# A 16384 x 2048 x 2048 product: B22 also by quarters, the next A11 B11 inside the A22 T4 block, PSUM as eight one-bank tiles, new slots for C

## The chip, the cores and the metric

One core of one Trainium2 chip. The metric is the device time of one execution in microseconds (us), the median of several runs. All runs told here were classed fast (but for the single one of `before_again`, whose state is unknown), so they are compared as they stand; a "slow" or "typical" run below is only the longer one of several fast ones. "The first kernel" below is the kernel before the change, "the changed kernel" the one after it.

In the lines of the profile PE is TensorE (PEld its weight loads), DVE VectorE, ACT ScalarE, POOL GpSimd and SP the engine that issues the transfers (DMAs). PSUM is the memory that TensorE writes its sums to; a bank of it holds one 128x512 tile in fp32. An eviction is the read of such a tile out of PSUM.

## The reference

```python
def setup_inputs():
    B, S, D = 8, 2048, 2048
    return {"x": np.random.randn(B, S, D).astype(np.float32),
            "w": np.random.randn(D, D).astype(np.float32)}

def reference(x, w):
    cs = np.cumsum(x, axis=1)
    diff = cs - np.concatenate([np.zeros(...), cs[:, :-1, :]], axis=1)
    return np.matmul(diff, w).astype(np.float32)
```

The difference of the running sum is x itself, so the kernel computes x (16384 x 2048) times w (2048 x 2048).

## The kernel before

The rows come in tiles of 128. Two row tiles make a pair, and a pair of row tiles with the halves of w is multiplied in Winograd's form of Strassen's scheme: seven products of half size in place of eight. In the code A11, A12 are the halves of the first row tile, A21, A22 those of the second; B11 to B22 are the quarters of w; S1 to S4 and T1 to T4 are sums of A and of B. One `product` is 16 matmuls of 128x512. Two pairs make a group (pair g and pair h); there are 31 groups. The first is "plain": it runs while the operands of the inner level are still being made.

In the other 30 groups some products are split once more ("by quarters"): pair g's A and pair h's A are taken as the two row blocks of an inner scheme. Seven inner products of 4 matmuls, 28 in all, take the place of two products of 16, 32 in all. The first kernel does this for A12 B21 of both pairs (`inner_2`) and for A22 T4 of both pairs (at the end). Every sum of products passes through an add in fp32 on VectorE, from PSUM into the output tile C.

```python
    cpool = ctx.enter_context(tc.tile_pool(name="C", bufs=4))
    psum4 = ctx.enter_context(tc.tile_pool(name="ps4", bufs=1, space=bass.MemoryType.PSUM))

    def product(ps, a, b, first):
        for k in range(KH):                                  # 8
            for n in range(NH // NB):                        # 2
                nc.tensor.matmul(ps[:, ds(n * NB, NB)], a[k], b[k][:, n, :],
                                 start=(first and k == 0), stop=(k == KH - 1), ...)

    def product_in(ps, a, b, first):
        for k in range(4):
            nc.tensor.matmul(ps, a[k], b[k], start=(first and k == 0), stop=(k == 3), ...)

    def keep(dst, ps, scale):                                # eviction on ScalarE
        after("act", lambda: nc.scalar.activation(dst, ps, COPY, scale=scale))

    def add(dst, ps, scale):                                 # eviction on VectorE
        after("dve", lambda: nc.vector.scalar_tensor_tensor(dst, ps, scale, dst, MUL, ADD))

    # less_in: the sums of an inner scheme's operands, 16 subtractions on VectorE
    # weigh: |x| summed over a row (ScalarE); ready: narrow to 16 bits, transpose by DMA

    def group(t0, X, Y, Z, V):                # X, Y, Z, V: PSUM tiles 128x1024, two banks
        g, h = t0, t0 + 2
        q, e = V[:, :NB], V[:, NB:]
        early = g == PLAIN
        # ... weigh(h + 1), ready(h + 1), units, sums_in(A12g, A12h)

        def inner_2():
            y, z = Z[:, :NB], Z[:, NB:]
            product_in(q, a11, t11, True)
            add(Cg[:, :NB], q, ug)
            product_in(y, a12, t21, True)
            add(Cg[:, :NB], y, ug)
            product_in(e, s1, Q1, True)
            product_in(q, s2, Q2, False)
            add(Cg[:, NB:], q, ug)
            # ... weigh(g + 4), ready(g + 4); s4 t22 and a22 Q4 with their adds
            product_in(q, s3, Q3, False)
            add(halves(Ch), both(q), uh)
            put(Ch, h, 0)

        product(X, A11g, B11, True); Cg = new_c(); keep(Cg, X, ug)
        # ... (the plain group: product(V, A12g, B21, True), less(T3, ...), sums(g), add)
        product(Y, A11h, B11, True); Ch = new_c(); keep(Ch, Y, uh)
        # ... (the others: sums(g), inner_2())

        def rest(t, X, S):
            S1, S2, S3, S4 = S
            product(X, S2, T2, False); C12 = new_c(); keep(C12, X, u0)
            product(Z, S1, T1, True);  C22 = new_c(); keep(C22, Z, u1)
            # ... weigh, ready
            product(X, S3, T3, False); add(C22, X, u1)
            put(C22, t + 1, 1)
            product(Z, S4, B22, False)                     # 16 matmuls for each pair
            add(C12, Z, u0)
            put(C12, t, 1)

        # ... sums(h), units; in the plain group also less(T4, ...) and less_in(in2)
        rest(g, X, Sg)
        # ... in the second group less_in(in4); sums_in(A22g, A22h)
        rest(h, Y, Sh)

        # A22 T4 of both pairs, by quarters
        product_in(q, a11, t11, True);          keep(Cg[:, :NB], q, vg)
        product_in(X[:, :NB], a12, t21, False)
        product_in(e, s1, Q1, True)
        product_in(q, s2, Q2, False);           keep(Cg[:, NB:], q, vg)
        # ...
        product_in(q, s3, Q3, False);           keep(halves(Ch), both(q), vh)
        add(Ch[:, NB:], e, vh); add(Ch, Y, vh); put(Ch, h + 1, 0)
```

## Time and profile before

| | first kernel |
|---|---|
| median of 3 runs | 1556.03 us (1555.99 to 1556.76) |
| TensorE busy | 1522.0 us, 98% of the span, 7020 matmuls |
| VectorE, ScalarE busy | 55%, 53% |
| one steady group | 46.69 us, 216 matmuls |
| waits of TensorE after the first 160 us | under 1 us in all |

Read it from the top: one engine is busy nearly all the time, its waits are nearly all at the start, and its pitch (0.2158 us a matmul) does not vary. The time is then the number of matmuls times the pitch, plus the start and the end. The lines behind this stand in the prediction.

### The profile page before, as it was taken

Reading aid. Unit: us, or ns where it says so; the run is one execution under the profiler, and the core shown is the slowest. Engines: PE = TensorE matmul, PEld = TensorE weight load, DVE = VectorE, ACT = ScalarE, POOL = GpSimd, SP = SyncE. Lnnn points to the kernel's source line nnn. Section 1 sums busy time; section 2 is a strip of 40 time slices with the busy share of each in tenths; the row PEclk is TensorE's granted clock in tenths of the full one; section 3 lists DMA queues with packets and bytes.
Section 4 is the critical chain, followed back from the end, with each engine's and each line's share of the span. In section 5 each row is a group of like instructions: output and inputs, shape, how many; then the busy total and the mean of one; then the engine's idle time right before and its main releaser. Section 6 shows DMA issues by size and latency. Waiting matters only on the chain.

```text
span 1555.1 us, 18082 instructions
## 1 busy us (share of the span) xinstructions
PE 1522.0 (98%) x7020; PEld 689.8 (44%) x7024; DVE 854.0 (55%) x1477; ACT 823.2 (53%) x712; POOL 7.3 (0%) x16
## 2 busy tenths in 40 slices
PE   6979999999999999999999999999999999999998
PEld 3434444444444444444444444444444444444443
DVE  5866656555456555456555456554456554456553
ACT  5774455555455555455555455555455555455541
POOL 0100000000000000000000000000000000000000
PEclk9999999999999999999999999999999999999999
DMA  9868777877777867777877777777777877777852
GB/s 360 316 176 247 219 224 226 247 209 232 214 226 222 249 210 231 215 226 220 247 213 232 215 228 218 247 213 232 216 227 216 247 214 232 216 228 215 247 171 98
DMA packets 319221, 351.41 MB, mean 226 GB/s; under 512 B 264736, under 2 KB 264736, under 8 KB 303136
## 3 DMA queue, kind: packets, MB, share of 16 engines
q1 hardware_dynamic: 317968, 346.07, 73.2%
q0 software_dynamic: 1168, 4.19, 0.7%
q8 instruction: 55, 0.90, 0.2%
q14 instruction: 30, 0.25, 0.0%
HBM read 150.99 MB, written 134.22 MB: 183 GB/s over the span
## 4 chain that ended last, share of the span: by engine, by line
PE 90%; DVE 0%; ACT 0%; issue 0%
PE Y L336 22%; PE X L336 22%; PE Z L336 22%; PE V L347 13%; PE X L347 3%; PE Z L347 3%; PE Y L347 3%; DVE c L375 0%; DVE W L384 0%; ACT c L371 0%; DVE xT L384 0%; DVE u L426 0%; DVE m L111 0%; DVE s L112 0%; ACT xT L105 0%
## 5 line engine op out<-in xcount | busy, mean ns | idle before, releaser
L336 PEld LDWEIGHTS <-W 128*128 128x128 f16 x2976 | 291.2, 98 | 351.2
L116 ACT ACTIVATE fin<-fin,s 128x2048 f16<-128x2048 f32 x124 | 248.2, 2002 | 130.8 <-issue 98.4
L336 PEld LDWEIGHTS <-xT 128*128 128x128 f16 x2048 | 200.8, 98 | 249.1 <-issue 9.1
L375 DVE SCALAR_TENSOR_TENSOR c<-V,u,c 128x512 f32<-128x512 f32 (+1 forms) x211 | 174.7, 828 | 185.9 <-ACT c L371 115.2
L105 ACT ACTIVATE xT<-fin 128x2048 f16<-128x2048 f32 x124 | 235.9, 1903 | 21.6 <-PE X L347 6.1
L336 PE MATMUL Z<-W,W 128*128 128x512 f16 x896 | 217.2, 379 | 0.0
L336 PE MATMUL X<-W,W 128*128 128x512 f16 x854 | 207.5, 379 | 0.0
L336 PE MATMUL Y<-W,W 128*128 128x512 f16 x854 | 207.5, 379 | 0.0
L371 ACT ACTIVATE c<-V,u 128x512 f32<-128x512 f32 (+1 forms) x90 | 74.6, 829 | 189.6 <-PE V L347 189.6
L336 PE MATMUL Y<-W,xT 128*128 128x512 f16 x688 | 157.2, 382 | 2.7 <-DMA xT<-fin 2.7
L336 PE MATMUL X<-W,xT 128*128 128x512 f16 x688 | 155.7, 379 | 2.4 <-DVE m L111 1.8
L375 DVE SCALAR_TENSOR_TENSOR c<-Y,u,c 128x1024 f32<-128x1024 f32 (+1 forms) x91 | 100.6, 1106 | 86.7 <-PE Y L336 47.9
L336 PE MATMUL Z<-W,xT 128*128 128x512 f16 x656 | 148.3, 379 | 0.0
L375 DVE SCALAR_TENSOR_TENSOR c<-Z,u,c 128x1024 f32<-128x1024 f32 (+1 forms) x93 | 103.2, 1110 | 81.5 <-PE Z L336 42.6
L347 PEld LDWEIGHTS <-W 128*128 128x128 f16 x960 | 93.7, 98 | 116.1 <-issue 6.4
L375 DVE SCALAR_TENSOR_TENSOR c<-X,u,c 128x1024 f32<-128x1024 f32 (+1 forms) x91 | 100.7, 1106 | 79.1 <-PE X L336 40.2
L111 DVE TENSOR_SCALAR m<-m 128x1 f32<-128x1 f32 x124 | 18.2, 147 | 227.7 <-ACT xT L105 227.7
L371 ACT ACTIVATE c<-Y,u 128x1024 f32<-128x1024 f32 x63 | 69.9, 1110 | 125.2 <-PE Y L336 125.2
L371 ACT ACTIVATE c<-X,u 128x1024 f32<-128x1024 f32 x63 | 70.0, 1110 | 120.5 <-PE X L336 118.9
L371 ACT ACTIVATE c<-Z,u 128x1024 f32<-128x1024 f32 x62 | 68.8, 1110 | 111.1 <-PE Z L336 111.1
L347 PE MATMUL V<-in,W 128*128 128x512 f16 x480 | 113.3, 379 | 0.3 <-DVE c L375 0.3
L347 PEld LDWEIGHTS <-xT 128*128 128x128 f16 x720 | 70.4, 98 | 85.0
(67 smaller groups left out, 1048.1 us busy)
## 6 DMA issues: line engine op xcount, KB each, us to landing
fin<-in_x_dram SPq DMA_DIRECT2D x125, 1024.0 KB, 6.6
out_dram<-c SPq DMA_DIRECT2D x248, 512.0 KB, 4.3
W<-in_w_dram SPq DMA_DIRECT2D x32, 512.0 KB, 9.7
out_dram<-o POOLq DMA_DIRECT2D x7, 512.0 KB, 3.8
W<-in_x_dram SPq DMA_DIRECT2D x12, 256.0 KB, 7.8
xT<-fin SPq DMA_TRANSPOSE x124, 4.3
out_dram<-o POOLq DMA_DIRECT2D x2, 256.0 KB, 4.1
```

The source lines that it names most:

```text
L105: return m, xT, nc.scalar.activation(xT.rearrange("p k m -> p (k m)"), xf, ABS, accum_out=m)
L111: nc.vector.tensor_scalar(m, m, TINY, 1.0 / ROW, MAX, MUL)
L116: return xh, nc.scalar.activation(xh, xf, COPY, scale=s)
L336: nc.tensor.matmul(ps[:, ds(n * NB, NB)], a[k], b[k][:, n, :], start=(first and k == 0), stop=(k == KH - 1), skip_group_check=True,)
L347: nc.tensor.matmul(ps, a[k], b[k], start=(first and k == 0), stop=(k == 3), skip_group_check=True)
L371: after("act", lambda: nc.scalar.activation(dst, ps, COPY, scale=scale))
L375: "dve", lambda: nc.vector.scalar_tensor_tensor(dst, ps, scale, dst, MUL, ADD)
```

## The change

Its intent: S4 B22 of the two pairs is also taken by quarters in 30 of the 31 groups, which saves 4 of 216 matmuls. This gives VectorE and ScalarE more to do, so the order is redone around it: PSUM becomes eight tiles of one bank each, so that a write to one bank never has to wait for a read of its neighbour; the A22 T4 block has its inner products in another order, with the next group's A11 B11 put between two of them; x tiles are weighed into a slot of C, and one of four into PSUM; C's slots are assigned by name.

```diff
+    def bank(i):
+        return psum.tile([P, NB], f32, name=f"b{i}")
@@ weigh: the waste goes into a slot of C, or (weigh_in) into two banks of PSUM
+            m, _ = after("act", lambda: measure(xf, new_c(slot)))
@@ product, keep, add: a list of two one-bank tiles in place of a two-bank tile
-                    ps[:, ds(n * NB, NB)],
+                    ps[n],
...
@@ rest: only the plain group keeps it; the others
+        product(X, S2, T2, False)
+        C12g = new_c(c)
+        keep(C12g, X, ug)
...
+        product(Z, S1, T1, True)
+        C22 = new_c(d)
+        keep(C22, Z, vg)
+        add(C12g, Z, ug)
...
+        inner_product(A2, in2, banks, C11g, C11h, *u, between_2)
...
+        if second:
+            less_in(*in3)
+        one, two, A3 = sums_in(S4g, S4h, S0, S3g)
...
+        inner_product(A3, in3, banks, C12g, C12h, *u, between_3)
+        put(C12h, h, 1)
...
+        if second:
+            less_in(*in4)
+        product(Y, S3h, T3, False)
...
@@ A22 T4, at the group's end
+        product_in(q, s2, Q2, False)
+        add(C21g[:, NB:], q, vg)
+        put(C21g, g + 1, 0)
+        weigh(h + 5, d)
+        if g + 4 < END:
+            product(X, parts(g + 4)[0], B11, True)
+        add(C21h[:, NB:], e, vh)
+        product_in(q, s3, Q3, False)
```

## The prediction

> **What bounds the kernel now.** I read the page's busy line first, then who made TensorE wait over the whole run, then three stretches of 140 us from the middle, then the order of single instructions.
>
> ```profile
> PE 1522.0 (98%) x7020; PEld 689.8 (44%) x7024; DVE 854.0 (55%) x1477; ACT 823.2 (53%) x712; POOL 7.3 (0%) x16
> ...
> PE 90%; DVE 0%; ACT 0%; issue 0%
> ```
>
> TensorE is busy 98% of the span and carries 90% of the chain that ended last. A busy PE need not be a PE at its best, so I checked two more things. First, what it waited for in all (us in total, times, longest):
>
> ```profile
> PE V L151 <- POOL eye masks.py:199: 10.6, 1, 10.6
> PE X L266 <- ACT W L245: 4.5, 5, 2.8
> PE Y L336 <- DMA xT<-fin: 2.7, 1, 2.7
> PE V L266 <- ACT W L245: 2.4, 3, 1.5
> PE X L336 <- DVE m L111: 1.8, 1, 1.8
> ...
> PE V L347 <- DVE c L375: 0.3, 1, 0.3
> ```
>
> All of these lie in the first 160 us (start-up, and the first group, which does without the inner level). Second, the pitch: in the chain a product of 16 matmuls takes 3.45 us, so one 128x512 matmul takes 0.2158 us, and that is the same in all three stretches, at full clock:
>
> ```profile
> 184.40:324.48 140.08, 140.08 (x649) 63.38 (x648) 75.13 (x132) 74.21 (x63) 0.00 (x0) 1.00 0.75 225
> 604.63:744.70 140.07, 140.07 (x650) 63.42 (x648) 75.12 (x132) 74.22 (x63) 0.00 (x0) 1.00 0.75 225
> ```
>
> The columns are PE, PEld, DVE, ACT, POOL busy, clock, DMA share and GB/s. Such a stretch holds three groups of two row pairs, 648 = 3 x 216 weight loads; with as many matmuls a group takes 140.08 / 3 = 46.69 us. The code says the same: two pairs of seven products of 16 are 224, less 4 where A12 B21 of both pairs is taken by quarters (7 x 4 = 28 for 2 x 16 = 32), less 4 for A22 T4. 216 x 0.2158 = 46.61, so only 0.08 us of a group is not matmuls at full pitch. Where it goes can be seen at a group's last inner products:
>
> ```profile
> 702.37 0.69 ACT L371 ACTIVATE c<-V,u 128x512 f32<-128x512 f32 x1 [2.30 <-PE V L347]
> 702.82 0.10 PEld L347 LDWEIGHTS <-W 128*128 128x128 f16 x1
> 703.11 1.89 PE L347 MATMUL V<-in,W 128*128 128x512 f16 x8
> ```
>
> The next product starts 703.11, just after the ACT read of V's first bank ends (703.06), though it writes V's second bank; at pitch it would have started at 702.17 + 4 x 0.2158 = 703.03. So the kernel is bound by the number of its matmuls, and DVE (75.13 / 3 = 25.0 us of 46.7 a group) and ACT (24.7 us) have room.
>
> **What the Trainium skill says.** "TensorE: Matmul & The Clock Gate", section "Back-to-back issue gap", gives N / 2.4 + 2.5 ns warm, 216 ns for N = 512; the trace agrees (215.8). (The section also gives about 131 ns for a sustained stream of 512-wide matmuls, which this trace doesn't show.) "PSUM — Partial Sum Buffer", section "PSUM bank collisions raise a hardware error", says two engines may not be in one bank and quadrant at once, reads against reads included. That concerns the change: keep(C22, Z) on ACT and add(C12, Z) on DVE now read the same Z banks after one product, so they must take turns; the trace of before has no such pair. "ScalarE: Activation LUTs", section "What ACT_TABLE_LOAD costs", gives an ACTIVATE a fixed part (186 ns, and 93 for each pointer operand) beside 0.833 ns an element, and 93 ns of overlap back to back. The trace agrees nearly: 687 ns for 512 and 1110 for 1024. An eviction in two halves is then dearer, 2 x 687 less 93 = 1281 against 1110.
>
> **The change part by part.**
>
> 1. Matmuls. In 30 of the 31 groups S4 B22 of both pairs goes from 2 x 16 to 7 x 4 = 28 matmuls: 4 fewer a group, 120 in all, at 0.2158 us = 25.9 us. All of that lies on the path that sets the end. A group should take 212 x 0.2158 = 45.75 us.
> 2. One-bank tiles. The wait of 0.08 us a group goes, since the bank written is no longer in the tile being read: 30 x 0.08 = 2.4 us. Moving A22 T4 to the group's end, with the next A11 B11 between (s2 Q2) and (s3 Q3), puts 3.45 us of other work between them and hides the read of their shared bank q.
> 3. DVE gets dearer. From the costs by shape:
>
> ```profile
> L375 DVE SCALAR_TENSOR_TENSOR c<-V,u,c 128x512 f32<-128x512 f32 x180 | 134.9, 750 | 150.6 <-ACT c L371 115.2 <-PE V L347 34.3
> L375 DVE SCALAR_TENSOR_TENSOR c<-Z,u,c 128x1024 f32<-128x1024 f32 x63 | 80.9, 1284 | 76.6 <-PE Z L336 42.6 <-ACT xT L105 31.9
> L384 DVE TENSOR_TENSOR W<-xT 128x512 f16<-128x512 f16 x61 | 25.4, 416 | 0.0
> ```
>
> A group gets a third inner block (7 adds of 0.75 and one of 1.28: 6.5 us), four adds of 1.284 each in two of 0.75 (+0.9), four more sums of 0.42 (+1.7), the last folds (+0.2) and one reduce (+0.2): 25.0 + 9.5 = 34.5 us, 75% of 45.75. Beside PE, if it comes in time.
> 4. ACT: 16 evictions of 0.69 = 11.0 us for the former 9.2, and one of the four ABS passes in four pieces into PSUM (about 3.2 for 2.1): 24.7 + 3 = 27.7 us, 61%. Not on the path.
> 5. One-time costs, estimated by following the program's order with these durations. Plain group: the sums of the second pair now stand behind the first pair's last add on DVE and have one set of S1, S2 slots, so PE waits about 0.2 + 1.4 + 0.2 + 1.4 = 3.2 us for S2; the 1.8, 0.6 and 0.3 us waits of before in that group go. The 2.7 us wait for the first transposes stays. About +0.5. Second group: the weighing and narrowing of a row tile stand ahead of the eviction of the first X (+1.5), and 32 operand subtractions instead of 16 come here (+1). Together +3.
> 6. The end. The last matmul of before (slot end 1547.9) is followed by three dependent steps:
>
> ```profile
> 1548.10 1.11 ACT L371 ACTIVATE c<-V,u 128x1024 f32<-128x1024 f32 x1 [1.90 <-PE V L347]
> 1549.24 0.75 DVE L375 SCALAR_TENSOR_TENSOR c<-V,u,c 128x512 f32<-128x512 f32 x1 [0.88 <-ACT c L371]
> 1550.03 1.28 DVE L375 SCALAR_TENSOR_TENSOR c<-Y,u,c 128x1024 f32<-128x1024 f32 x1
> ```
>
> After, one add of 1.28 us follows it: 1.9 us less; but in the last group nothing stands between (s2 Q2) and (s3 Q3), so PE waits about 1 us for the add between. Net -1.
>
> Sum: -25.9 - 2.4 + 3 - 1 = -26.3 us, 1529.7 us, were the steady groups free of new waits.
>
> **The rivals.**
>
> *DVE becomes the bound in the inner blocks.* In one, DVE has 7 adds and a wide one: back to back an add starts 0.66 us after the one before (721.01 and 721.67 in the timeline), so 7 x 0.66 + 1.28 = 5.9 us, for 28 matmuls of PE = 6.04 us. There is no room to catch up inside a block, and DVE enters the second and third blocks late, from add(C12, Z) that takes turns with ACT on Z and (second) three sums of 0.69 and add(C22, X). Following the order by hand, add q ends 0.3 to 0.45 us after PE wants bank q for (s2 Q2) in both blocks if reads take turns, 0.3 us before if they don't. At the worst 0.8 us a group, 30 x 0.8 = 24 us: the gain is gone, about 1554. Against it: PE's order is chosen when the program is built, and the timeline of before shows matmuls of the following product put between inner products, with no wait left. The product after each of the two blocks (Y S2 T2, Y S3 T3) is ready in time to do so.
>
> *A wait for a slot of C.* The ABS pass now writes its waste into a slot of C and waits for that slot's store to land, and DVE waits in order for its result before the block's last add. Stores take 4.3 us (median):
>
> ```profile
> out_dram<-c SPq DMA_DIRECT2D x248, 512.0 KB, 4.3
> xT<-fin SPq DMA_TRANSPOSE x124, 4.3
> ```
>
> By the order, C22's store starts about 15.5 us into a group, the slot is free near 20, the ABS result is there near 22.2, and DVE must have it by about 23.3: a margin of 1.1 us. Stores of 6 us would cost about 0.6 us a group, 18 us: about 1548. x tiles (two buffers) and transposes (even tiles in two buffers, odd ones in halves) come by 0.7 to 6 us before their use.
>
> *The gain is above the count.* If the one-time costs are hidden, -25.9 - 2.4 - 1.9 = -30.2: 1526. Over 2% needs 31.1 us, more than all I can name without also shortening the start-up.
>
> **Range and chances.** I put the remaining waits at 0.08 us a steady group (as before, elsewhere), +2.4 us: 1532. The lower end is the sum with all one-time costs hidden, 1526; the upper one has half of both rivals, 0.3 + 0.3 us a group, 18 us: 1549. Faster by over 2% (below 1524.9) needs something I haven't seen: 0.07. Slower by over 2% (above 1587) needs 1.9 us of waits a group, more than both rivals at their worst together: 0.03. Within 2%: 0.90.
>
> **What would show it.** Step 1: 6904 matmuls, 212 weight loads a group, PE pitch 0.2158. Steps 1 and 2: a group of 45.75 to 46.0 us and no wait of PE on ACT at inner products. Steps 3 and 4: DVE near 75%, ACT near 60% of a steady stretch. The first rival would show as PE L347 or its heir waiting for DVE c many times by 0.3 to 0.5 us; the second as ACT waiting for the DMA of out<-c and DVE m for ACT at the end of inner blocks. Step 5: waits on DVE W once near 125 us. Step 6: one 128x1024 add as the last compute. I would be wrong if a group took over 46.4 us or under 45.7.

## The result, and the profile after

The changed kernel took 1537.32 us in the median (1533.2, 1536.61, 1538.02, 1538.52), the first kernel 1556.32 us in the same rounds. The ratio is 0.9873, with a 95% interval of 0.9854 to 0.9892. Ratios here are the mean time of one kernel's fast runs over the mean of the other's of the same rounds, so not quite the ratio of the medians quoted. The change is faster, clear of the noise, but by less than 2%.

The profiled run is the fastest of the four (1533.2 us). The page's busy line:

```profile
PE 1494.6 (98%) x6904; PEld 677.0 (44%) x6904; DVE 1095.2 (72%) x2036; ACT 868.9 (57%) x1109; POOL 6.7 (0%) x15
```

The 6904 matmuls are those counted in advance. TensorE is still the bound, with 84% of the chain that ended last. VectorE rose from 55% to 72% and did not become it, as what TensorE waited for shows (us in total, times, longest):

```profile
PE b L282 <- ACT W L260: 7.2, 7, 3.4
PE b L338 <- DMA xT<-fin: 3.4, 1, 3.4
PE b L349 <- DVE c L385: 2.9, 6, 0.8
```

L349 is the inner product. It waited for VectorE six times in the whole run. From 215 us on all waits of TensorE come to 1.1 us. The busy times of stretches of the changed kernel (columns PE, PEld, DVE, ACT, POOL, clock, DMA share, GB/s) show where the even course begins:

```profile
151.78:201.41 49.63, 47.04 (x214) 20.48 (x212) 41.45 (x92) 25.00 (x33) 0.00 (x0) 1.00 0.69 190
201.41:249.19 47.78, 46.34 (x212) 20.65 (x213) 34.16 (x65) 27.01 (x37) 0.00 (x0) 1.00 0.85 236
...
612.67:750.08 137.41, 137.41 (x638) 62.22 (x636) 98.83 (x186) 78.64 (x103) 0.00 (x0) 1.00 0.81 230
```

Three steady groups take 137.41 us, so one takes 45.80 us for 212 weight loads, 0.89 us less than before. The first two groups with quarters (groups 2 and 3) take 49.63 and 47.78 us, 5.8 us too much together. In the first kernel the same two lost next to nothing; group 3 took the steady 46.69 us, and group 2 (columns as above):

```profile
147.52:193.97 46.45, 46.16 (x214) 20.82 (x213) 28.08 (x58) 24.62 (x21) 0.00 (x0) 1.00 0.79 233
```

What happens there is in the order of single instructions of the changed kernel (start, length, engine, line, operation; in brackets the idle time before and what ended it):

```profile
188.38 1.42 DVE L398 TENSOR_TENSOR inner<-W 128x512 f16<-128x512 f16 x4
...
193.75 2.71 DVE L385 SCALAR_TENSOR_TENSOR c<-b,u,c 128x512 f32<-128x512 f32 x4
194.54 1.02 PE L349 MATMUL b<-inner,xT 128*128 128x512 f16 x4 [0.59 <-DVE c L385]
...
206.92 0.60 ACT L434 ACTIVATE b<-fin 128x512 f32<-128x512 f32 x1 [3.38 <-DMA fin<-in_x_dram]
...
209.38 2.40 ACT L380 ACTIVATE c<-b,u 128x512 f32<-128x512 f32 x4
...
210.10 3.75 PE L338 MATMUL b<-W,xT 128*128 128x512 f16 x16 [1.31 <-ACT c L380]
```

L398 is `less_in`: 5.4 us of subtractions (from 188.38) stand in VectorE's queue ahead of the adds at 193.75 that free the banks, and TensorE waits. These lines are two of about a dozen such places; counted by the starts of the matmuls, the largest single loss of the two groups is the 1.5 us at 210.10. The delay travels on: VectorE's late work makes the next transposes late, these make the next x tile late, and ScalarE's weighing of that tile (L434) stands ahead of the eviction (L380) which TensorE needs at 210.10. The chain of waits there runs through the same two DMAs, one behind the other: a transpose (3.44 us from 197.13) and the x tile (6.20 us from 200.63).

The end of the changed kernel:

```profile
1525.20 0.38 PE L349 MATMUL b<-W,W 128*128 128x512 f16 x1 [0.84 <-DVE c L385]
...
1526.26 1.28 DVE L385 SCALAR_TENSOR_TENSOR c<-b,u,c 128x1024 f32<-128x1024 f32 x1 [0.46 <-PE b L349]
```

One wide add is the last compute, and TensorE waits 0.84 us between (s2 Q2) and (s3 Q3).

**Where the time went.** I counted matmuls from the start of each trace: 544 up to the end of the plain group, then 216 or 212 a group. Beside the fastest run of the changed kernel stands a typical one (`again`, below, 1537.3 us):

| stretch | first kernel | changed, fastest run | changed, typical run |
|---|---|---|---|
| up to the 544th matmul | 147.3 | 144.7 | 147.9 |
| groups 2 and 3 | 93.8 | 97.4 | 98.7 |
| groups 4 to 30 | 1260.7 | 1237.0 | 1236.6 |
| group 31 and the end | 53.3 | 52.4 | 52.3 |
| span | 1555.1 | 1531.4 | 1535.5 |

The steady groups give the gain that the count promises; groups 2 and 3 give 4 to 5 us of it back; the fastest run differs from the typical one before group 4, but for 0.4 us in the other direction.

### The profile page after: what moved, and what is told of

Its sections match the earlier page's. It is cut to its first block, busy times and chain, and to the rows that moved or that the text cites. A ratio compares the mean times of both kernels' runs of the same rounds, so it can differ in the third digit from the quotient of the medians.

```text
span 1531.4 us, 19075 instructions
## 1 busy us (share of the span) xinstructions
PE 1494.6 (98%) x6904; PEld 677.0 (44%) x6904; DVE 1095.2 (72%) x2036; ACT 868.9 (57%) x1109; POOL 6.7 (0%) x15
## 4 chain that ended last, share of the span: by engine, by line
PE 84%; DMA 1%; DVE 1%; ACT 0%; issue 0%; SPq 0%; ACTq 0%; DVEq 0%
PE b L338 50%; PE b L349 34%; DMA fin<-in_x_dram 1%; DMA xT<-fin 1%; DVE c L385 0%; ACT b L434 0%; DVE W L394 0%; ACT c L380 0%; DVE u L467 0%; SPq L128 0%; DVE m L442 0%; DVE m L112 0%; DVE s L113 0%; DVE xT L394 0%; ACTq L434 0%
## 5 line engine op out<-in xcount | busy, mean ns | idle before, releaser
L385 DVE SCALAR_TENSOR_TENSOR c<-b,u,c 128x512 f32<-128x512 f32 (+1 forms) x882 | 674.6, 799 | 237.2 <-ACT c L380 109.3
L338 PE MATMUL b<-W,xT 128*128 128x512 f16 x2048 | 463.0, 379 | 5.4 <-DMA xT<-fin 3.4
L380 ACT ACTIVATE c<-b,u 128x512 f32<-128x512 f32 x496 | 315.0, 680 | 266.9 <-PE b L338 170.9
L338 PE MATMUL b<-W,W 128*128 128x512 f16 x1764 | 411.6, 379 | 0.1
L106 ACT ACTIVATE c<-fin 128x2048 f16<-128x2048 f32 x93 | 177.6, 1910 | 252.0 <-DMA out_dram<-c 216.1
L338 PEld LDWEIGHTS <-xT 128*128 128x128 f16 x2048 | 200.3, 98 | 247.7 <-DMA xT<-fin 3.9
L338 PEld LDWEIGHTS <-W 128*128 128x128 f16 x2016 | 197.1, 98 | 240.9 <-DVE W L394 4.0
L349 PEld LDWEIGHTS <-W 128*128 128x128 f16 x1560 | 152.1, 98 | 189.1 <-issue 3.8
L349 PE MATMUL b<-W,W 128*128 128x512 f16 x810 | 220.2, 379 | 1.3 <-DVE c L385 1.3
L349 PE MATMUL b<-W,xT 128*128 128x512 f16 x720 | 180.0, 379 | 0.7 <-DVE c L385 0.7
L349 PE MATMUL b<-inner,W 128*128 128x512 f16 x660 | 176.4, 379 | 0.4 <-DVE c L385 0.3
L349 PEld LDWEIGHTS <-xT 128*128 128x128 f16 x960 | 93.9, 98 | 114.9 <-issue 1.9
L338 PE MATMUL b<-W 128*128 128x512 f16 x252 | 75.1, 379 | 2.2 <-DVE W L394 2.2
L434 ACT ACTIVATE b<-fin 128x512 f32<-128x512 f32 x116 | 68.0, 586 | 15.0 <-DMA fin<-in_x_dram 14.8
L394 DVE TENSOR_TENSOR W<-W,xT 128x1024 f16<-128x1024 f16 x122 | 68.1, 558 | 3.2
L394 DVE TENSOR_TENSOR W<-xT,W 128x1024 f16<-128x1024 f16 x122 | 67.3, 552 | 0.0
L349 PE MATMUL b<-inner,xT 128*128 128x512 f16 x240 | 61.6, 379 | 0.6 <-DVE c L385 0.6
```

Of the source, the lines that this page charges most:

```text
L106: return m, nc.scalar.activation(waste.bitcast(f16), xf, ABS, scale=1.0 / ROW, accum_out=m)
L338: nc.tensor.matmul(ps[n], a[k], b[k][:, n, :], start=(first and k == 0), stop=(k == KH - 1), skip_group_check=True,)
L380: after("act", lambda: nc.scalar.activation(c, p, COPY, scale=scale))
L385: "dve", lambda: nc.vector.scalar_tensor_tensor(c, p, scale, c, MUL, ADD)
L394: after("dve", lambda: nc.vector.tensor_tensor(dst.all, p.all, q.all, op))
L434: lambda: nc.scalar.activation(ps[i % 2], xf[:, at], ABS, scale=1.0 / ROW, accum_out=m4[:, i : i + 1],),
```

## The experiments

Twelve kernels, in three calls. The kernels of a call ran on one chip, another for each call, with the first kernel beside them (1555.76, 1556.32 and 1556.07 us). All gave correct results.

### again: the changed kernel unchanged

No edit. The question was what makes one run 1533 and another 1538.

> The changed kernel as it is, to see what its runs from 1533.2 to 1538.5 us are. Theory A (clock at the start): every slow run has a lower mean granted clock (0.993 to 0.994 for 0.997), and in a slow run's trace the loss lies before 140 us; steady groups stay at 45.80 us. Theory B (late DMAs): the time does not go with the clock, and a slow trace shows TensorE waits of 0.3 us and more in some steady groups, behind a late x tile. Both: median 1534 to 1538.

Measured: 1537.12 us (1533.73, 1536.94, 1537.3, 1537.5), ratio 0.9872 (0.9857 to 0.9886). The profiled run this time is a slow one, and its steady group is 45.80 us as well, with 0.8 us of waits after 215 us: late DMAs in the steady groups (Theory B) are refuted for this trace. The mean clock does not separate the runs: 1536.94 and 1537.5 had .997, the fastest .997 too. In windows of 8 us the clock does show:

```profile
88.00:96.00 8.00, 7.88 (x28) 2.70 (x26) 3.09 (x7) 7.75 (x10) 1.06 (x2) 0.77 0.94 323
96.00:104.00 8.00, 4.65 (x20) 1.84 (x18) 7.91 (x16) 3.15 (x3) 0.00 (x0) 0.87 0.69 178
```

Column 6 after the stretch, ahead of the last two, is the clock. In the fastest run the same two windows had 0.97 and 1.00. That is a part of the difference; at 64 us, before any of these windows, the slow run was already 10 matmuls behind (243 against 253), 2.2 us at full pitch. Nor was the clock on the fastest run's side throughout: from 64 to 72 us it had 0.79, and the slow run 1.00. So Theory A holds for a part only.

### warm: TensorE kept at work through the two long idle stretches of the start

```diff
@@ product of the late row tile, after the V block and again after product(V, A12g, B21)
+                    spin = bank(2)
+                    with tc.issue_after(said.ins):
+                        for k in range(14):
+                            nc.tensor.matmul(spin, late_x[:, 0, :], B11[0][:, 0, :], start=True, stop=True)
```

> 28 matmuls of no use, 14 in each of the two start-up waits of 3.4 us near 80 and 97 us, so that TensorE is not idle there. Theory A (the low clock after those waits costs time and makes the runs differ): the clock is 1.00 from 80 us on, the mean granted clock rises to 0.998 and more in all runs, the median falls by 1.5 to 3 us, to 1534 to 1535.5, and the runs lie within 3 us. Rival: the spread is of the DMAs in the first 60 us, the median and the spread stay (1537, 4 to 5 us).

The Trainium skill, "TensorE: Matmul & The Clock Gate", section "Part 1: The HAM clock gate (the "warmup" mystery)", says that an idle window of about 3.4 us takes the clock to half, that a busy one of that length brings it back, and that the window runs freely, so that the effect varies from run to run. Measured: 1535.02 us (1533.63 to 1537.3), ratio 0.986 (0.9843 to 0.9876). In the two windows above the clock now stayed up, as the page leads one to expect of an engine kept busy:

```profile
88.00:96.00 8.00, 6.66 (x29) 2.70 (x28) 3.44 (x9) 7.53 (x10) 1.06 (x2) 1.00 0.94 330
96.00:104.00 8.00, 7.60 (x36) 3.31 (x35) 7.91 (x14) 2.67 (x3) 0.00 (x0) 1.00 0.66 163
```

That filling the two waits keeps the clock up in these windows is thus shown. But it was not 1.00 from 80 us on, as I had expected: in this trace it was 0.86 from 120 to 128 us and 0.93 from 128 to 136, after the wait of 2.01 us that the plain group still has (at 125.47 us here). The median is 2.1 us lower, within what was expected, but the intervals of the two ratios overlap and the runs still spread by 3.7 us (3 or less expected), so the size of the gain in time is not settled by this run; `best`, below, speaks against it.

### s4_whole: the new order without the saving

```diff
-        inner_product(A3, in3, banks, C12g, C12h, *u, between_3)
+        product(V, S4g, B22, True)
+        add(C12g, V, ug)
+        between_3(2)
+        product(Z, S4h, B22, True)
+        add(C12h, Z, uh)
@@ and less_in(in3) and the sums for A3 left out
```

> S4 B22 again as two products of 16, all else as changed. If the gain is matmuls alone, a group takes 4 x 0.2158 = 0.86 us more (46.66 us) and the time is 1563 us (+26), DVE's share of a steady stretch falls from 72% to about 57%. If the third inner block costs waits as well (DVE as the bound), the time rises by less than 20 us.

Measured: 1557.37 us (1556.5 to 1559.33), ratio to the first kernel 1.0008 (0.9993 to 1.0023). 7024 matmuls, and a steady group (1226.77 to 1273.42 us) takes 46.65 us for 216 weight loads, where 46.66 were expected; VectorE's share of it is 61% (28.36 us), where 57% were. All of the steady gain therefore comes with the 120 matmuls; the new order by itself is worth nothing here. The whole time rose by 20.2 us and not 26, because this kernel also lacks a part of the loss in groups 2 and 3: they take 96.2 us, 2.9 over two steady groups, against 7.0 in `again`.

### no_gap_forced: (s3 Q3) right behind (s2 Q2)

```diff
-        if g + 4 < END:
-            product(X, parts(g + 4)[0], B11, True)
         add(C21h[:, NB:], e, vh)
-        product_in(q, s3, Q3, False)
+        said = product_in(q, s3, Q3, False)
+        if g + 4 < END:
+            with tc.issue_after(said.ins):
+                product(X, parts(g + 4)[0], B11, True)
```

> The product X A11 B11 of the next group is forced behind the (s3 Q3) product instead of between (s2 Q2) and (s3 Q3). My theory: TensorE then waits for the DVE add between the two in each group, as at the end of the changed kernel (0.84 us): 29 x 0.84 = 24 us, 1561 us. Rival: the move is worth nothing, because other matmuls are put in between or DVE is early: under 3 us.

Measured: 1546.37 us (1541.52 to 1548.34), ratio 0.994 (0.9924 to 0.9957). A steady group takes 46.01 us, 0.21 more than in the changed kernel, a quarter of what I expected, and no wait of 0.84 us appears in the steady groups. In the timeline of TensorE in this kernel:

```profile
1163.47 1.03 PE L349 MATMUL b<-inner,W 128*128 128x512 f16 x4
1164.41 1.39 PE L338 MATMUL b<-W,xT 128*128 128x512 f16 x5
```

The matmuls did not run in the order in which the program writes the products: five matmuls of a following product (L338) stand in the gap though the program wrote nothing there. (I take it that this order is settled when the program is built; no run here shows where.) Most of what I credited to the product between is done without it. Per group it is worth 0.21 us, some 6 us over the steady groups; most of the rest of the 9 us lies in groups 2 and 3 (100.3 us here, against 97.4 and 98.7), where TensorE once waits 4.12 us, at 195.06 us, for VectorE's adds behind the subtractions.

### pair_tiles: all of the group's PSUM as two-bank tiles

```diff
-    banks = [bank(i) for i in range(8)]
-    banks = [banks[i : i + 2] for i in range(0, 8, 2)]
+    psum2 = ctx.enter_context(tc.tile_pool(name="ps2", bufs=1, space=bass.MemoryType.PSUM))
+    banks = [psum2.tile([P, NH], f32, name=n) for n in "XYZV"]
+    banks = [[t[:, :NB], t[:, NB:]] for t in banks]
```

> PSUM of the groups in four two-bank tiles again, evictions still in halves. My step 2 says 0.08 us a group and more, as three inner blocks have reads of one bank beside writes of the other: with fills between, 0.1 to 0.4 us a group, 1540 to 1549 us. Rival: the fills hide all of it, 1537 us, and the one-bank tiles are worth nothing.

Measured: 1653.32 us (1652.67 to 1654.64), ratio 1.0624 (1.0608 to 1.064). A steady group takes 49.47 us, 3.67 more: far outside what I expected. TensorE's waits and the timeline of this kernel, in the third inner block and the start of the fourth:

```profile
PE V L349 <- DVE c L385: 44.4, 34, 1.5
PE V L349 <- DVE m L110: 13.3, 29, 1.5
```

```profile
1039.19 0.74 DVE L385 SCALAR_TENSOR_TENSOR c<-V,u,c 128x512 f32<-128x512 f32 x1
...
1039.98 1.02 PE L349 MATMUL V<-W,xT 128*128 128x512 f16 x4 [0.42 <-DVE m L110]
...
1041.04 1.28 DVE L385 SCALAR_TENSOR_TENSOR c<-V,u,c 128x1024 f32<-128x1024 f32 x1 [0.86 <-PE V L349]
...
1042.38 1.02 PE L349 MATMUL V<-W,xT 128*128 128x512 f16 x4 [1.38 <-DVE c L385]
```

By the program's order the add at 1039.19 reads e, the second bank of V, and (s3 Q3) at 1039.98 writes q, the first. They are different banks, but the wait follows the tile: the matmuls start as the add ends (1039.93). The late (s3 Q3) makes the wide add of q late (1041.04), and the fourth block, which writes q next, waits 1.38 us for it. The two engines take turns.

### pair_v and pair_xyz: which of the tiles carries it

The edit of `pair_tiles` for V alone, and for X, Y and Z alone.

> Only V is a two-bank tile again, X, Y and Z stay as one-bank tiles. In pair_tiles V had 58 of some 85 us of the waits listed. If V's waits are its own: a group costs about 2.5 us more than 45.80, so about 48.3 us and 1610 us in all. Rival: the waits in V are only where a delay made elsewhere (X, Y, Z) comes to light; then V alone costs under 0.5 us a group, and the time is under 1553 us.

> X, Y and Z are two-bank tiles, V stays two one-bank tiles. If V carries the loss of pair_tiles: a group costs about 1 us more than 45.80, so about 46.8 us and 1565 us in all. Rival (X, Y, Z carry it): about 3 us more a group, 48.8 us and about 1625 us.

Measured: pair_v 1574.67 us (1572.81 to 1576.38), ratio 1.0117 (1.0102 to 1.0132); pair_xyz 1568.21 us (1567.41 to 1569.53), ratio 1.0078 (1.0061 to 1.0095). Over 26 steady groups pair_v takes 46.92 us a group (+1.1), pair_xyz 46.90 (+1.1), pair_tiles 49.56 (+3.75). The number for pair_xyz was hit, that for pair_v (48.3) missed, and with it the theory; its rival (under 0.5 us a group) missed too. V has most of the waits to its name and is not the main cause. X, Y and Z do not carry it alone either, as the rival had it. Each set of tiles costs about 1.1 us, and some 1.5 us more come only when both are there; why was not tested. A second thing is worth seeing: pair_xyz has no more than 2.1 us of listed waits from 400 to 1400 us, yet loses over 1 us in each group. In its timeline of TensorE

```profile
1037.40 1.03 PE L349 MATMUL X<-W,xT 128*128 128x512 f16 x4
...
1038.57 1.02 PE L349 MATMUL V<-W,xT 128*128 128x512 f16 x4
```

four matmuls take 1.17 us from start to start in place of 0.86. Such a gap of 0.3 us is too short to be listed as a wait, as the modelled end of a matmul lies 0.16 us past its slot. A group's length shows such losses, the list of waits does not.

### before_v_banks: the first kernel with V as two one-bank tiles

```diff
-        return (psum4 if name == "V" else psum).tile([P, NH], f32, name=name)
+        if name == "V":
+            return [psum4.tile([P, NB], f32, name=f"v{n}") for n in range(2)]
+        return psum.tile([P, NH], f32, name=name)
```

> The kernel before with V alone as two one-bank tiles. My step 2 said the 0.08 us a group goes with this: group 46.61 us, 30 x 0.08 = 2.4 us, 1553.4 us. Rival: the wait was not the tile's, the group stays 46.69 us and the time 1555.8 us.

Measured: 1553.32 us (1552.89 to 1554.47), ratio 0.9982 (0.9967 to 0.9996), and a steady group (238.65 to 285.27 us of its trace) of 46.62 us against 46.69: the wait of 0.08 us a group seen in the first kernel was this one, and one-bank tiles remove it.

### before_again: the first kernel, unchanged

> The kernel before once more, for a second trace: steady groups of 46.69 us again; the first 145 us differ from the first trace by up to 3 us, as its runs do (1555.0 to 1558.2).

1556.26 us, groups of 46.69 us. The reference has not moved.

### early_in: the subtractions one group earlier

```diff
@@ group_plain, after the last A22 T4
+        less_in(*in3)
@@ second group: less_in(in3) and less_in(in4) taken out of the inner blocks
+        if second:
+            less_in(*in4)          # after the first sums, ahead of turn(h + 1)
```

> The 16 operand subtractions for B22 are put at the end of the plain group on DVE and the 16 for T4 right after the first sums of the second group, instead of beside the second group's inner blocks. In the traces of the changed kernel the second and third group take 49.6 and 47.8 us instead of 45.8, 5.8 us together. If that is the subtractions and the late x tile that follows from them, both groups come to within 1 us of 45.8 and the median falls from 1537 by 4 to 6 us, to 1531 to 1533. Rival: the groups lose the time to something else (the first passes of the C slots and transposes), less than 2 us gained.

Measured: 1531.33 us (1527.65 to 1534.75), ratio 0.9839 (0.9821 to 0.9856). Groups 2 and 3 of this kernel:

```profile
155.05:201.29 46.24, 45.92 (x213) 20.63 (x212) 37.03 (x77) 26.02 (x35) 0.00 (x0) 1.00 0.84 226
201.29:247.09 45.80, 45.80 (x213) 20.73 (x212) 32.95 (x63) 26.19 (x35) 0.00 (x0) 1.00 0.80 224
```

They lose 0.44 us in place of 5.8, and the median is 6.0 us below that of the changed kernel. The two are from different calls, and the runs of this one spread by 7.1 us; but against the first kernel of its own call it gains 25.0 us, where the changed kernel gained 19.0 and 18.6. That the subtractions' place in VectorE's queue caused the loss is thus shown: they are all still made, only earlier.

### early_both: the sums of the plain group's second pair earlier too

```diff
@@ rest of the first pair, between keep(C22, Z, u1) and product(X, S3, T3)
+            if early:
+                early.append(sums(t + 2, S4h))
```

> As early_in, and besides the sums for S2 and S3 of the plain group's first pair are made one product earlier, while TensorE still has a whole product of matmuls that do not need them. My theory: the single wait of 2.01 us of the plain group (a matmul waiting for VectorE's W, at about 124 us) goes, so 1531.3 - 2.0 = about 1529.3 us, and no wait for W of over 0.5 us is left between 110 and 140 us. Rival: the order of the build fills that time anyway or the sums push the eviction of an earlier product back, and the time stays at 1531 us with a new wait in the same stretch.

The wait is the one that the changed kernel shows in the plain group, and `early_in` still has, at 127.41 us and of the same length:

```profile
124.14 0.60 PE L338 MATMUL b<-W 128*128 128x512 f16 x2 [2.01 <-DVE W L394]
```

Measured: 1530.08 us (1527.44 to 1530.96), ratio 0.9828 (0.9813 to 0.9842). The wait is gone, but in group 2 TensorE now waits 1.07 us for ScalarE's eviction at 161.02, where it did not before. About half comes back. The median is 1.3 us below that of `early_in`, which is less than the runs of either spread. It was run on another chip.

### best: all three together

`early_both` with the 28 matmuls of `warm`.

> All that was found to help together: the subtractions one group earlier, the sums one product earlier, and the matmuls without use that fill the two long idle stretches of the start. If the gains add: 1531.3 - 2.0 - 2.1 = about 1527.2 us, between 1525 and 1529, faster than both kernels, with a clock of 1.00 in all windows from 64 us on and a spread of runs of at most 5 us. If they do not add (the warm matmuls' gain being in the same stretch as the earlier sums): 1529 to 1531 us.

Measured: 1529.85 us (1528.86 to 1530.95), ratio 0.9829 (0.9814 to 0.9844). It is 26 us below the first kernel and some 7 us below the changed one, but no better than `early_both`: the gains do not add, and the lower figure I had for it (1527.2) fails. The spread is 2.1 us. The clock was 1.00 from 80 us on, but 0.82 in the window 64 to 72, ahead of the matmuls added. Part of what was won in the start was lost in group 2:

```profile
154.52 1.27 ACT L388 ACTIVATE c<-b,u 128x512 f32<-128x512 f32 x2 [4.55 <-DVE inner L406]
...
158.13 2.41 ACT L388 ACTIVATE c<-b,u 128x512 f32<-128x512 f32 x4
...
158.85 0.38 PE L345 MATMUL b<-W,xT 128*128 128x512 f16 x1 [1.71 <-ACT c L388]
```

ScalarE's eviction at 158.13 comes after its weighing of an x tile there, and TensorE, arriving earlier, waits 1.71 us for it (1.07 in `early_both`). The weighing in turn came after an eviction that began only at 154.52. The profile puts that one down to VectorE; but a store out of C, issued at 146.9 us, landed after 7.5 us, just before it, and in `early_in` the same eviction waits 2.32 us for such a store by name. So the wait for a slot of C, the prediction's second rival, probably costs TensorE time here; no run tested it.

## Why the prediction was right or wrong

The prediction, 1532.0 us, was 5.3 us under the median and within its range. (One slip in the range: half of the first rival's 0.8 us is 0.4 and not 0.3, which puts the upper end some 3 us higher.) Its mechanism, the number of matmuls, was right. By its own steps:

1. *Matmuls.* Right. 6904 matmuls, 212 weight loads a group, the same pitch; `s4_whole` gives the 4 matmuls back and lands at 46.65 us a group.
2. *One-bank tiles and the product between.* The first half is right in size for the first kernel (`before_v_banks`: 46.62 for 46.69). Three things were wrong. I gave one-bank tiles 0.08 us a group, which is what the wait cost in the first kernel; in the new order, where three inner blocks follow each other closely, two-bank tiles cost 3.67 us a group, four times the whole gain. One-bank tiles were not a small extra, they are a condition of the change. The product between (s2 Q2) and (s3 Q3) does not hide a whole wait: it is worth 0.21 us a group, since matmuls of another product fill the gap without it. And A22 T4 was not moved to the group's end, as I wrote: it stood there in the first kernel.
3. *VectorE.* Right in kind. 98.83 / 3 = 32.9 us a group, 72% of it, where 34.5 and 75% were predicted. It did not become the bound: the first rival (0.3 to 0.45 us for each block) is refuted by the group of 45.80 us. The reads of the Z banks did take turns: in a steady group ScalarE's two evictions start at 639.29 us (0.68 us each), and VectorE's add, after 2.66 us of waiting for ScalarE, at 640.01; but TensorE did not wait for it.
4. *ScalarE.* Right: 26.2 us a group where 27.7 was predicted. The second rival, the wait for a slot of C, exists but costs nothing in the steady groups: ScalarE waited 216.1 us in all for stores out of C (49 times), VectorE 48.0 us for the weighing behind it, and TensorE for neither in the steady groups. Stores landed in 3.1 us (median; before 4.3), so the margin I had worked out from 4.3 was larger than thought.
5. *One-time costs.* This is the term that was mis-sized. The wait for S2 was right in kind (2.01 us, 3.2 predicted), and the plain group ends 0.6 us later in the typical run (+0.5 predicted), 2.7 earlier in the fastest. But for the second group I put 2.5 us in all (1.5 for the weighing ahead of the first eviction, 1 for the subtractions), and groups 2 and 3 together lost 5.8 in the fastest and 7.0 in the typical trace. The weighing cost nothing in these traces at the place I had named. The subtractions cost more, because I counted only VectorE's own delay of a bank and not the chain behind it: transposes, x tile, weighing, eviction, into group 3. `early_in` removes it, and with it 6.0 us.
6. *The end.* Right: 0.9 us less (1 predicted), with a wait of 0.84 us (about 1) between (s2 Q2) and (s3 Q3).

The remaining waits, 0.08 us a group (+2.4), came to 45.80 - 45.75 = 0.05. Set against the first kernel, the typical run's sum is +0.6 (start) + 4.8 (groups 2 and 3) - 24.1 (27 groups) - 0.9 = -19.6 us. The prediction had -24. What remains open is the spread of some 2 to 7 us between runs of one kernel: of the 4.1 us between the two traces of the changed kernel 3.2 arise in the first 150 us, the clock has a part in it, and the part before 64 us was not pursued.

## What to carry to other kernels

Where one engine is full, count its instructions and the time follows; but follow what an engine with room is given to do once through its queue to the DMAs it releases, as one late block there gave back what six groups save. A buffer's division decides what must wait for what: V as a two-bank tile cost 0.08 us a group in one order and 1.1 us in another, and all four tiles so 3.7 us. The name in a list of waits says where a delay shows, not where it starts, and a loss of 1 us a group can hide from that list altogether, so measure a group's length.

## What the Trainium skill lacked or had wrong

- "TensorE: Matmul & The Clock Gate", section "Back-to-back issue gap": it gives about 131 ns a matmul as the sustained figure for 512-wide ones and calls the formula (216 ns) that of isolated matmuls. Here a stream of weight loads and 512-wide matmuls ran at 215.8 ns for over 1300 us in both kernels. (Other passages of the page give 215.7 ns back to back, which agrees.)
- The same page, section "Part 1: The HAM clock gate (the "warmup" mystery)": its table of the two states asks for an idle window of about 3.4 us before the clock halves. Here a matmul that had waited 2.67 us (first kernel) was followed by 16 matmuls in 5.30 us in place of 3.62, and in `warm` a wait of 2.01 us that ended at 125.47 us by a clock of 0.86 (120 to 128 us) and 0.93 (128 to 136), so shorter waits can do it; and of two waits of nearly equal length, one (the changed kernel, 3.39 us) was followed by 32 matmuls at full pitch and one (`early_in`, 3.37 us) by 32 in 8.57 us. The last agrees with what the page says of a window that runs freely. The lines, first kernel, changed kernel, `early_in`:

```profile
100.86 5.30 PE L336 MATMUL Y<-W,xT 128*128 128x512 f16 x16 [2.67 <-DMA xT<-fin]
```

```profile
100.65 7.08 PE L338 MATMUL b<-W,xT 128*128 128x512 f16 x32 [3.39 <-DMA xT<-fin]
```

```profile
102.43 8.57 PE L338 MATMUL b<-W,xT 128*128 128x512 f16 x32 [3.37 <-DMA xT<-fin]
```

- "PSUM — Partial Sum Buffer", section "PSUM bank collisions raise a hardware error": it says that different banks do not collide, and to guard by bank and quadrant. It lacks that a program's waits can be coarser than that: here they followed the PSUM tile as allocated, over two banks, at 0.08 us a group in the first kernel and 3.67 us a group in `pair_tiles`.
- No page that I read says that a gap in TensorE's work can be filled with matmuls of a product which the program writes later: five of them in `no_gap_forced`, which took the cost of the missing product between from an expected 0.84 to 0.21 us a group.
